# An attention kernel: loads of the first pass wait for the landing of the fourth load ahead of them

## Chip, cores and metric

The kernel runs on one core of one Trainium2 chip. The metric is the device time of one execution in microseconds (us); the time before is 235.31 us, the median of 3 runs (234.92 to 235.79). Engines are named as in the profile: PE multiplies matrices (PEld is its loading of weights), ACT applies functions, DVE is the vector engine, POOL and SP are the two engines that also issue most of the DMAs here. Transfers that POOL issues convert fp32 in memory to bf16 on the chip; those of SP copy without converting.

## What is computed

Softmax attention with one additive bias for all heads: 4 batches of 8 heads, 1024 positions, head size 64, all in fp32 at the interface.

```python
scores = scale * np.matmul(q, k.transpose(0, 1, 3, 2))
scores = scores + bias
scores_max = np.max(scores, axis=-1, keepdims=True)
attn = np.exp(scores - scores_max) / (np.sum(np.exp(scores - scores_max), axis=-1, keepdims=True) + 1e-8)
return np.matmul(attn, v).astype(np.float32)
```

## The kernel before

The 32 heads are worked on in 16 pairs. A query chunk is 128 rows, so each head has 8 chunks, and a unit of work (a "slot" in the code) is one chunk of one head: 256 slots. A slot has these steps.

- fill (lines 233 to 249): PE puts the 128 x 1024 scores of the slot into one of three places in PSUM, in 8 multiplications (L244). Where a chain of heads begins, the bias is put there first (L241, from `braw`); later heads of the same chunk add the difference of their scores to what stands there, so that the bias need not be added again. For this each pair keeps arrays `ko`, `qo` and `ke`, `qe` (k and q of one head, and of two heads one below the other, with the sign of one q turned).
- exponential (L258): ACT reads the place and writes `E` in bf16 (15 buffers). For 19 of the slots DVE does this instead in six steps (L275 to L295); 238 instructions of ACT remain.
- product with v (L312): PE multiplies `E` by `vall`, which holds v with a column of ones. Up to seven such results share a bank; then DVE divides them (L320, L322) and SP stores them (L689). There are two such banks, `xa` and `xb`, and the transposes use them too.

Heads go in two groups of 7 and 9 pairs. A group passes over its heads with chunks 0, 1 and 2 first, then with chunks 3 and 4, then with the rest. The first pass of the first group begins when the kernel begins: it takes pairs 0 to 6 one after the other, and each pair's k, q and v must have come by then.

How an input gets ready: a load brings k, q or v of one pair (each 256 KB as bf16; q of pairs 0 and 1 in two parts, the second named `qrest`) or 128 rows of the bias. PE transposes k and q (L191), DVE copies the result to `ko` or `qo` (L199, L201) and doubles it to `ke` and `qe` (L210, L212), or SP copies half of it with a DMA (L539). DVE copies v to `vall` (L493). There are 5 landing buffers for k, 5 for q, and 3 for v.

The order of all instructions is written out ahead by a planner in the kernel (from line 394 on), which carries an estimated time for each engine and picks what comes next. Each engine runs its list in order.

The loads: q, k and bias chunk 0 of the very beginning come by SP and ACT. POOL then issues seven loads directly (lines 352 to 358: bias chunks 1 and 2, k and q of pair 1, v of pair 0, k and q of pair 2). After these, line 767 calls `early` for 21 loads, in this order: k3, q3, v1, k4, q4, v2, k5, q5, v3, k6, q6, v4, v5, b3, q0, b4, v6, q1, b5, b6, b7 (b is a chunk of the bias, q0 and q1 are the second parts of q of pairs 0 and 1). `early` calls `issue`, which appends to the list `flight` the last element of what is loaded together with an estimated landing time. All 21 are issued by POOL ahead of everything that POOL does later.

Loads of pairs 7 to 15 come from `load` and `next_v`, by `issue` with `depth` LATE = 2 (3 for the last v loads). With a depth, `issue` puts a copy of one element ahead of the load (L468): it reads the last element of the load that many places back in `flight` and writes it to `tick`, so POOL waits until that load has landed.

```python
if 0 < depth <= len(flight):
    what, t = flight[-depth]
    nc.gpsimd.tensor_copy(tick[:], what)
```

With depth 0, as `early` calls it, there is no such copy.

Of the kernel before, what the change touches and what calls it, by code (L numbers as in the profile page):

```python
# [16 lines left out]
def kernel(  # L17
# [13 lines left out]
    nc = tc.nc  # L31
# [39 lines left out]
    tick = consts.tile([1, 1], BF)  # L71
# [263 lines left out]
    with tc.manual_schedule():  # L335
# [98 lines left out]
        flight = []  # L434
# [28 lines left out]
        def issue(at, cost, depth, load, pr, *a):  # L463

            nonlocal t_dma
# [3 lines that stand above are left out]
                at = max(at, t + 100)  # L469
            at = pool(at, 750)  # L470
            t_dma = max(t_dma + cost, at + 2200 + cost)
            flight.append((load(pr, *a), t_dma + 200))
            return t_dma + 200
# [17 lines left out]
        def move_v(pr):  # L491
            def run(t2):
                nc.vector.tensor_copy(vall[:, 2 * pr % VR:2 * pr % VR + 2, :, :D], lands[pr, "v"][:])  # L493
                v_at[pr] = t2 + 480 + L_DVE
                next_v(v_at[pr])
            dve_q.append((vland_at[pr] + VSLACK * (pr >= EARLY), 0.3, 480, run))


        def early(kind, pr):
            if kind == "k":  # L500
                raw_at[pr, 1, 0] = issue(0, E1, 0, load_k, pr) + SLACK
            elif kind == "q":
                cs = slice(0 if pr >= SPLIT else C0, NCH)
                raw_at[pr, 0, cs.start] = issue(0, E1 if pr >= SPLIT else E2, 0, load_q, pr, cs) + SLACK
            elif kind == "v":
                vland_at[pr] = issue(0, E1 if pr < 5 else E2, 0, load_v, pr)
                move_v(pr)
            else:
                bias_at[pr] = issue(0, E2, 0, load_b, pr)
# [257 lines left out]
        for x in ("k3", "q3", "v1", "k4", "q4", "v2", "k5", "q5", "v3", "k6", "q6", "v4", "v5", "b3", "q0", "b4", "v6", "q1", "b5", "b6", "b7"):  # L767
            early(x[0], int(x[1]))
# [71 lines left out]
```

## Time and profile before

| | |
|---|---|
| median of 3 runs | 235.31 us (234.92 to 235.79) |
| profiled execution, its own time | 235.12 us |
| its span, first to last instruction | 233.4 us |
| granted clock of PE, mean | 0.996 |
| DVE busy | 197.7 us, 290 instructions |
| POOL busy | 61.7 us, 99 instructions |
| exponentials on ACT (L258) | 238, 218.4 us busy |
| SP stores (L689), first pass, issue to landing | 2.6 / 6.2 / 8.6 us (min / median / max) |

How to read the profile: times count from the first instruction. A line of a timeline gives the start, the time from start to end of a row of merged instructions, the engine, the line of the code, the operation, what it writes and reads, the shape, how many there are, and in brackets the idle time of the engine before them with what ended it. "issue" as the one that ended it means that the profile shows nothing that the engine waited for. The digits after DMA are the mean busy share of the 16 DMA engines, in tenths, in 40 equal slices of the span. q0 is the queue of POOL's loads, q1 that of SP's and ACT's transfers, q8 that of instructions. Landing is when a DMA's data have arrived and its semaphore says so. POOL's DMA instructions are counted as busy while POOL writes their descriptors.

### The profile page before, as it was taken

How to read it: one execution, taken by the hardware profiler on the slowest of the kernel's cores; microseconds unless marked ns; L12 is line 12 of the kernel's file. 1: busy time of each engine (PE TensorE's matmuls, PEld its weight loads, DVE VectorE, ACT ScalarE, POOL GpSimd, SP SyncE). 2: the span in 40 equal slices, each digit the busy share in tenths (PEclk: the TensorE clock that was granted, in tenths of full speed). 3: DMA queues.
4: the chain of work that ended last, by engine and by line, in shares of the span. 5: the costliest groups of instructions: out<-in, count | busy, mean ns of one | idle time of the engine just before them, and what ended most of it. 6: DMA issues, size and time to landing. Idle time of an engine off the chain costs nothing.

```text
span 233.4 us, 10661 instructions
## 1 busy us (share of the span) xinstructions
PE 222.4 (95%) x4671; PEld 209.6 (90%) x4671; DVE 197.7 (85%) x290; ACT 221.6 (95%) x242; POOL 61.7 (26%) x99
## 2 busy tenths in 40 slices
PE   7899998899999999999999999999999999999992
PEld 2779997899999999998999999999998999999991
DVE  3576777599988998889989789899999899999991
ACT  3699999899999999999999999999999999999992
POOL 8754540276563636304254010000000000000000
PEclk9999999999999999999999999999999999999998
DMA  6999999899997999989899764111111112112112
GB/s 207 207 206 218 221 226 215 180 112 142 171 173 119 139 188 149 181 188 138 148 234 232 162 108 128 37 37 42 42 40 43 45 42 75 49 31 80 44 37 62
DMA packets 55645, 29.75 MB, mean 127 GB/s; under 512 B 31728, under 2 KB 51952, under 8 KB 55600
## 3 DMA queue, kind: packets, MB, share of 16 engines
q0 software_dynamic: 30336, 14.06, 48.5%
q1 hardware_dynamic: 24544, 14.33, 22.0%
q10 hardware_dynamic: 720, 0.69, 1.1%
q8 instruction: 36, 0.59, 1.1%
q14 instruction: 9, 0.07, 0.1%
HBM read 29.36 MB, written 8.39 MB: 162 GB/s over the span
## 4 chain that ended last, share of the span: by engine, by line
PE 44%; ACT 29%; issue 14%; DVE 5%; DMA 4%; SPq 2%; POOL 1%; DVEq 0%; ACTq 0%; POOLq 0%
ACT E L258 29%; PE pl L244 25%; PE po L312 12%; PE px L191 4%; DMA braw<-in_bias_dram 2%; PE pl L241 2%; SPq L689 2%; DMA out_dram<-ob 1%; DVE ob L322 1%; PE px L187 1%; DVE df L280 1%; DVE dy L275 1%; DVE dt L290 0%; DVE df L287 0%; DVE rs L320 0%
## 5 line engine op out<-in xcount | busy, mean ns | idle before, releaser
L258 ACT ACTIVATE E<-pl 128x1024 bf16<-128x1024 f32 (+1 forms) x238 | 218.4, 1119 | 3.4 <-PE pl L244 3.0
L312 PE MATMUL po<-vall,E 128*128 128x65 bf16 x1896 | 91.9, 194 | 1.7 <-ACT E L258 0.9
L312 PEld LDWEIGHTS <-E 128*128 128x128 bf16 x1896 | 77.4, 98 | 2.8 <-ACT E L258 1.2
L244 PE MATMUL pl<-qo,ko 128*128 128x128 bf16 x1024 | 76.9, 219 | 1.1 <-ACT E L258 0.6
L244 PEld LDWEIGHTS <-ko 128*128 128x128 bf16 x1160 | 69.4, 98 | 3.9 <-issue 0.9
L244 PE MATMUL pl<-qe,ke 128*128 128x128 bf16 x888 | 66.2, 219 | 2.1 <-issue 0.7
L244 PEld LDWEIGHTS <-ke 128*128 128x128 bf16 x888 | 53.4, 98 | 4.9 <-issue 1.3
L275 DVE TENSOR_SCALAR dy<-pl 128x1024 int32<-128x1024 f32 x19 | 23.2, 1221 | 4.4 <-PE pl L244 3.6
L322 DVE TENSOR_TENSOR ob<-po,rs 128x448 f32<-128x448 f32 (+2 forms) x39 | 23.2, 594 | 2.3 <-DVE rs L320 0.4
L284 DVE SCALAR_TENSOR_TENSOR dt<-df 128x1024 f32<-128x1024 f32 x19 | 23.2, 1220 | 0.3
L295 DVE SCALAR_TENSOR_TENSOR de<-dy,dt 128x1024 uint16<-128x1024 int32 x19 | 23.2, 1219 | 0.2
L287 DVE SCALAR_TENSOR_TENSOR df<-dt,df 128x1024 f32<-128x1024 f32 x19 | 23.1, 1220 | 0.1
L290 DVE SCALAR_TENSOR_TENSOR dt<-df,dt 128x1024 f32<-128x1024 f32 x19 | 23.1, 1219 | 0.1
L138 POOL DMA_DIRECT2D q<-in_q_dram x18 | 16.4, 911 | 7.0 <-DVE rs L320 5.4
L165 POOL DMA_DIRECT2D v<-in_v_dram x16 | 11.3, 705 | 20.9 <-DVE rs L320 9.9
L199 DVE COPY ko<-px 128x1024 bf16<-128x1024 bf16 (+1 forms) x16 | 10.8, 672 | 6.6 <-PE px L191 6.2
L201 DVE TENSOR_SCALAR qo<-px,sgn 128x1024 bf16<-128x1024 bf16 (+2 forms) x18 | 12.4, 686 | 4.2 <-PE px L191 2.6
L320 DVE RECIPROCAL rs<-po 128x7 f32<-128x7 f32 (+3 forms) x40 | 7.9, 197 | 7.2 <-PE po L312 7.0
L280 DVE TENSOR_SCALAR df<-dy 128x1024 f32<-128x1024 uint16 x19 | 13.3, 700 | 0.1
L241 PE MATMUL pl<-ident,braw 128*128 128x128 bf16 x136 | 11.6, 229 | 0.4 <-DMA braw<-in_bias_dram 0.3
L145 POOL DMA_DIRECT2D k<-in_k_dram x15 | 10.7, 713 | 2.2 <-DMA k<-in_k_dram 1.2
L241 PEld LDWEIGHTS <-braw 128*128 128x128 bf16 x136 | 9.9, 149 | 0.7 <-DMA braw<-in_bias_dram 0.5
(54 smaller groups left out, 119.9 us busy)
## 6 DMA issues: line engine op xcount, KB each, us to landing
v<-in_v_dram POOLq DMA_DIRECT2D x16, 256.0 KB, 6.1
k<-in_k_dram POOLq DMA_DIRECT2D x15, 256.0 KB, 6.3
out_dram<-ob SPq DMA_DIRECT2D x34, 96.0 KB, 3.6
ke<-ko SPq DMA_DIRECT2D x22, 128.0 KB, 4.7
out_dram<-ob SPq DMA_DIRECT2D x41, 64.0 KB, 2.3
q<-in_q_dram POOLq DMA_DIRECT2D x18, 128.0 KB, 4.9
qe<-q SPq DMA_DIRECT2D x17, 128.0 KB, 4.4
out_dram<-ob SPq DMA_DIRECT2D x67, 32.0 KB, 2.8
```

The costliest lines, as they stand in the source:

```text
L138: nc.gpsimd.dma_start(out=t[:, :, y, :], in_=(qf, kf)[x][pr][:, y].rearrange("p (c d) -> p c d", d=D))
L241: nc.tensor.matmul(to, braw[:, c, :].rearrange("p (kp kc) -> p kc kp", kc=NCH)[:, kc, :], ident8[:], start=i == 0, stop=False, skip_group_ ...
L244: nc.tensor.matmul(to, kk[:, kc, :], qq[:, c, :], start=False, stop=True, skip_group_check=True)
L258: nc.scalar.activation(e[:, i:i + n].rearrange("p b x -> p (b x)"), places[slots[s][0]][:, i:i + n].rearrange("p b x -> p (b x)"), ACTF.Ex ...
L275: w.tensor_scalar(t["y"][:], places[slots[s][0]].rearrange("p b x -> p (b x)"), scale * LOG2E * 65536.0, 127.0 * 65536.0, op0=ALU.mult, op ...
L280: w.tensor_scalar(t["f"][:], t["lo"], G / 65536.0, None, op0=ALU.mult)
L284: w.scalar_tensor_tensor(t["t"][:], t["f"][:], -G, t["f"][:], op0=ALU.add, op1=ALU.mult)
L287: w.scalar_tensor_tensor(t["f"][:], t["t"][:], Q, t["f"][:], op0=ALU.mult, op1=ALU.add)
L290: w.scalar_tensor_tensor(t["t"][:], t["f"][:], V, t["t"][:], op0=ALU.add, op1=ALU.mult)
L295: w.scalar_tensor_tensor(etile[s].bitcast(U16).rearrange("p c q -> p (c q)"), t["y"][:], 1.0 / 512.0, t["t"][:], op0=ALU.mult, op1=ALU.add)
L312: nc.tensor.matmul(po[:, j + i, :], etile[s][:, kc, :], vall[:, slots[s][2] % VR, kc, :], start=j + i + kc == 0, stop=kc == NCH - 1, skip_ ...
L322: nc.vector.tensor_tensor(ob[:, :n, :], po[:, :n, :D], rs[:, :n, :].to_broadcast([P, n, D]), op=ALU.mult)
```

## The change

In `early`, from the sixth call on, a copy of one element is put ahead of the load. It reads the last element of the load four places back in `flight`, so POOL waits until that one has landed before it issues the next. The order and the estimates of the planner are not touched.

```diff
         def early(kind, pr):
+            if len(flight) > 4:
+
+                nc.gpsimd.tensor_copy(tick[:], flight[-4][0])
             if kind == "k":
                 raw_at[pr, 1, 0] = issue(0, E1, 0, load_k, pr) + SLACK
```

`flight` holds only what went through `issue`; the seven loads of lines 352 to 358 are not in it.

## The prediction

> **What bounds the kernel now.** I read the page first, then the timeline of ACT, which shows what the end is made of.
>
> ```profile
> PE 222.4 (95%) x4671; PEld 209.6 (90%) x4671; DVE 197.7 (85%) x290; ACT 221.6 (95%) x242; POOL 61.7 (26%) x99
> ...
> DMA  6999999899997999989899764111111112112112
> ...
> q8 instruction: 36, 0.59, 1.1%
> ```
> ```profile
> 9.46 29.09 ACT L258 ACTIVATE E<-pl 128x512 bf16<-128x512 f32 x32 [0.67 <-PE pl L244]
> 38.86 1.94 ACT L258 ACTIVATE E<-pl 128x1024 bf16<-128x1024 f32 x2 [0.32 <-PE pl L244]
> 41.09 3.77 ACT L258 ACTIVATE E<-pl 128x1024 bf16<-128x1024 f32 x4 [0.29 <-ACT E L258]
> 45.51 4.89 ACT L258 ACTIVATE E<-pl 128x1024 bf16<-128x1024 f32 x5 [0.65 <-PE pl L244]
> 50.60 23.94 ACT L258 ACTIVATE E<-pl 128x1024 bf16<-128x1024 f32 x26 [0.20 <-PE pl L244]
> ```
>
> ACT makes 238 exponentials and sets the end: 26 in 23.94 us, the last one 1.02 long, is a pitch of 22.92 / 25 = 0.917 us, and 238 of them are 218 of the 233.4 us of the span. What can be won behind the start is only what ACT stands idle. Nearly all of that lies from 38.5 to 51 us. So I asked what PE did just before.
>
> ```profile
> 36.93 0.28 PEld L244 LDWEIGHTS <-ke 128*128 128x128 bf16 x5 [0.88 <-issue]
> 43.57 0.57 PEld L312 LDWEIGHTS <-E 128*128 128x128 bf16 x16 [0.94 <-issue]
> ```
> ```profile
> core 0: us, PE busy (x) PEld busy (x) DVE busy (x) ACT busy (x) POOL busy (x), PEclk, DMA share, GB/s
> 36.93:43.50 6.57, 5.86 (x127) 5.30 (x127) 3.98 (x9) 5.97 (x7) 0.00 (x0) 1.00 1.17 228
> ```
>
> PE's weight loads stop twice, the first time in the middle of a fill, with no semaphore to wait for ("issue"). Between the two stops lie 127 + 127 instructions and a wait or two, about 256. The page's instruction queue moved 0.59 MB in 36 packets, 16 KB each; 2 x 4671 instructions of PE over 36 packets is 260 to a packet. I read the stops as PE out of instructions: the next block comes late because it travels beside the loads. The trace's instruction packets of these two blocks begin at 34.48 and 41.25 and PE goes on 2.4 and 2.3 us after; counted in PE's instructions, the first five packets begin 18, 73, 90, 124 and 132 after a multiple of 256, later ones between 67 before and 66 after. From the two that stopped PE, 0.88 us at 24.5 ns each (6.3 us for 256) is 36, so some 90 is the latest that costs nothing.
>
> The loads themselves, POOL's timeline:
>
> ```profile
> 8.72 0.70 POOL L155 DMA_DIRECT2D q<-in_q_dram  x1
> 9.97 0.71 POOL L165 DMA_DIRECT2D v<-in_v_dram  x1 [0.55 <-DMA braw<-in_bias_dram]
> ...
> 13.07 0.70 POOL L165 DMA_DIRECT2D v<-in_v_dram  x1 [0.35 <-DMA v<-in_v_dram]
> ...
> 34.48 0.53 POOL L160 DMA_DIRECT2D braw<-in_bias_dram  x1 [0.78 <-DMA v<-in_v_dram]
> 44.41 0.18 POOL L468 COPY tick<-braw 1x1 bf16<-1x1 bf16 x1 [9.40 <-DMA braw<-in_bias_dram]
> 44.91 0.71 POOL L145 DMA_DIRECT2D k<-in_k_dram  x1 [0.32 <-PE pl L244]
> ```
>
> Already each load starts about 0.3 us behind the landing of the eighth ahead of it: v of pair 1 (9.97) behind the second bias load (3.84 + 5.8 = 9.7), v of pair 2 (13.07) behind v of pair 0 (5.77 + 7.0 = 12.8). Eight are in flight, each takes 9 to 11.7 us, and they land one by one: q of pair 3 at 8.72 + 9.3 = 18.0, the last bias load at 34.48 + 11.1 = 45.6, 19 landings in 27.6 us, 1.45 us each, 5.8 for four. The stage is bound by bandwidth (DMA share 1.17 above).
>
> **What the change adds.** `early` makes 21 loads; from the sixth (v of pair 2) on it puts a 1x1 copy on POOL first, so 16 copies, each with a wait for the landing four ahead. Nothing is removed or moved: the planner's times (`issue` with depth 0) are as before, so the order on PE, ACT, DVE and SP stays. It does act: v of pair 2 waits for 18.0 instead of 12.8 and starts some 5 us later, and so do the rest.
>
> Step 1, POOL's time. A copy takes 0.18 us free and up to 1.23 in later rows (59.62); with its wait met, copy and issue together took 0.82 (79.90 to 80.72) to 1.06 (73.54 to 74.60). That is under the 1.45 that a landing leaves, and POOL does nothing else here, so it costs nothing; without that cover it would be 16 x 0.3, about 5 us of later issue. The long copies ran beside DVE's two-input steps (59.59, 1.23 us, L290), which begin at 48.62; before, DVE's longest SBUF copies are 0.43 (L493), so at most 0.6 a copy. The Trainium skill (SBUF — State Buffer, section "SBUF: two separate sides") says that GpSimd and such DVE instructions lock each other out of a shared port pair for a whole instruction; the later rows agree, and by that rule too the sum here stays nothing.
>
> Step 2, when the loads land. A turn is: landing, copy, issue, landing. From landing to next issue the later stage took 0.6 (72.24 to 72.83) to 1.2 us (53.97 to 55.18); from a k load's issue to landing with at most two ahead 3.9 to 4.8. A turn is 4.5 to 6.0 against the 5.8 that four landings take anyway. I take 4.9 (the first pass has no long copies): the queue stays fed, and the landings stay where they are. Upper end: 0.2 late in each of four turns, 0.8 us at the last.
>
> Step 3, who waits. Behind the copies on POOL stand all later loads, the second stage's too (their first copy, 44.41, waits for a landing at 44.4). k and q have room: k of pair 4 lands at 20.7 and is transposed at 22.6, q of pair 6 31.0 and 37.3, k of pair 7 48.8 and 57.8; the biases land at 35.8 at the earliest and are used at 46.9. Only the v copies (L493) start as their load lands, and stand in DVE's order: 28.05 and 32.82 after idling 0.43 and 0.35. A v that is 0.2 to 0.4 late there (turns 1 and 2) is covered by the idle time DVE has just behind (0.43 before 28.91, 0.78 before 30.83, 0.33 before 34.98). I put down 0.1 us of ACT, 0 to 0.4.
>
> Step 4, what else uses the DMA engines. SP's half copies take
>
> ```profile
> DMA to landing us min/median/max: 5.2/6.3/8.3
> ```
> in the first pass (line 539, 14 to 45 us; eight loads in flight) and
> ```profile
> DMA to landing us min/median/max: 2.8/4.2/5.4
> ```
> from 46 to 90 us, with two or three. So what is in flight does delay other queues. The lateness of PE's blocks goes the same way: mean 87 instructions at eight, about -5 in the 14 from 44.8 to 122 us at two or three. No row shows four; a third of the way from -5 to 87 it is 26 on average, some 60 less than at eight, and 132 - 60 = 72 for the worst, under the 90. I take it that both stops of PE go, 1.82 us; the ends are none (0) and both. ACT's part of it: idle 0.32 + 0.29 + 0.65 = 1.26 by the list; by its pitch, the first exponential behind each gap costs some 0.1 more, 1.56. I take 1.4.
>
> Sum: 0.1 - 1.4 = -1.3 us on the profiled execution (235.12 us, span 233.4), 233.8; the median of the runs is 235.31, 0.19 higher, so 234.0.
>
> **Rivals.**
> B, nothing moves. The DMA engines have loads waiting at any moment, with four as with eight, and what another queue waits for may be its turn, not the depth. For it: SP's stores at 65 to 70 us took up to 6.3 us with few loads in flight; the 14.99 block was hardly late with eight. Against: the two medians above. PE stops as before: 235.3. The Trainium skill (DMA: Bandwidth & Descriptors, section "Queues, rings and completion order") speaks for it: each engine goes round its queues packet by packet, so a longer queue of loads would not hold up an instruction block longer. This trace disagrees so far as blocks came 1.5 us and more later than in the later stage, more than the 0.9 us that their own packet takes.
>
> C, slower: four in flight don't feed the engines. Place: v of pairs 3 to 5. It decides when a turn is over 5.8 us. With 1.2 from landing to issue and the 5.5 of the k load at 73.90, a turn is 6.7, 0.9 late a turn: v of pair 3 lands 0.9 late, of pairs 4 and 5 1.8. DVE stands at L493, the two evacuations behind it (33.50, 34.98) are late, PE has only two banks for them and the transposes, and ACT follows: 1.8 less the 0.33 of idle time, 235.3 + 1.5 = 236.8. Against it: the 1 us of room in step 2.
>
> **How the numbers follow.** The forecast 50%, 233.5 to 234.7; B 27%, 234.8 to 235.8; C 23%, 235.9 to 238. The likeliest gives 234.0. Range: down to 233.5 (both stops gone by the pitch, 1.56, and a little of the 0.3 us at 50.6), up to 236.4, half of C. Half a per cent, 1.18 us, is what a measurement can tell from no change: faster below 234.13 is most of the forecast, 40%; same the rest of it and B, 36%; slower C, with a little of B, 24%.
>
> **What would show it.** Right: no idle "issue" time on PE near 36.9 and 43.6; ACT without gaps from 10 to 50 us; loads in flight for 5 to 6 us instead of 10; the last bias load still landing near 45.6; SP's half copies under 6 us. Step 2 is wrong if that last landing is past 47 and L493 idles for over 1 us. Step 4 is wrong if PE's stops stay while the loads' time in flight halves. What I may have missed most easily is a new place for a late block.

## The result, and the profile after

The changed kernel is 0.5% slower: 235.93 us (median of 20 runs, 234.92 to 239.53) against 234.71 us of the kernel before (20 runs, 234.02 to 236.36); ratio 1.0048, 95% interval 1.0026 to 1.0069. A second series gave 236.03 against 235.05 us, ratio 1.0026 (1.0000 to 1.0052), the same way but with an interval that just reaches 1. Ratios here and below leave out executions more than 1.5% above the fastest of their kernel, so they are not exactly the quotients of the medians. The runs of the changed kernel spread far more than those of the kernel before. The profiled execution shown here took 234.92 us, one of its fastest, so its span of 232.8 us is no measure of the change; what can be read from it is where time is lost and won.

The timeline of ACT, changed kernel (start, length, engine, line, what, count, idle time before):

```profile
17.39 19.36 ACT L258 ACTIVATE E<-pl 128x1024 bf16<-128x1024 f32 x21 [0.41 <-PE pl L244]
37.28 3.80 ACT L258 ACTIVATE E<-pl 128x1024 bf16<-128x1024 f32 x4 [0.54 <-PE pl L244]
41.38 8.48 ACT L258 ACTIVATE E<-pl 128x1024 bf16<-128x1024 f32 x9 [0.30 <-ACT E L258]
```

PE's two stops without a semaphore are gone, and the gap of 0.65 us at 45.5 with them. In their place ACT idles 0.54 us at 37.28. (The 0.41 us at 17.39 stands behind q of pair 2, loaded ahead of all new waits; e7, which has none, idles 0.27 us there.) The timeline shows the chain that leads there, first DVE before, then DVE and PE after:

```profile
32.82 0.43 DVE L493 COPY vall<-v 128x1024 bf16<-128x1024 bf16 x1 [0.35 <-DMA v<-in_v_dram]
...
33.50 0.18 DVE L320 RECIPROCAL rs<-po 128x6 f32<-128x6 f32 x1
```

```profile
34.40 0.43 DVE L493 COPY vall<-v 128x1024 bf16<-128x1024 bf16 x1 [1.89 <-DMA v<-in_v_dram]
...
35.08 0.18 DVE L320 RECIPROCAL rs<-po 128x6 f32<-128x6 f32 x1
35.29 0.56 DVE L322 TENSOR_TENSOR ob<-po,rs 128x384 f32<-128x384 f32 x1
36.00 0.64 PE L191 MATMUL px<-ident,k 128*64 128x128 bf16 x16 [1.02 <-DVE ob L322]
```

Read the second from the bottom: PE stands 1.02 us before the transposes of k of pair 6, because the bank that they write is still to be evacuated; DVE evacuates late (35.08, 33.50 before), because it stood 1.89 us at the copy of v of pair 4, whose load lands at 34.4 (32.8 before). DVE stands again at v of pairs 5 and 6, 4.7 us at the v copies in all; it was 0.8 us.

The loads themselves, POOL's timeline of the changed kernel (L502 is the new copy):

```profile
24.08 0.18 POOL L502 COPY tick<-v 1x1 bf16<-1x1 bf16 x1 [0.38 <-DMA v<-in_v_dram]
24.53 0.70 POOL L145 DMA_DIRECT2D k<-in_k_dram  x1 [0.27 <-issue]
...
31.03 0.18 POOL L502 COPY tick<-k 1x1 bf16<-1x1 bf16 x1 [1.53 <-DMA k<-in_k_dram]
31.49 0.71 POOL L160 DMA_DIRECT2D braw<-in_bias_dram  x1 [0.28 <-issue]
```

A load starts 0.6 us behind the landing of the fourth ahead (23.95 to 24.53, 30.90 to 31.49) and is in flight for 4.5 to 8.4 us, 6.1 in the mean of the 16. A turn is 6.7 us. The landings say the same: q of pair 3 at 18.1, the last bias load at 49.4, 31.2 us for 19 landings, 6.6 us for four, where it was 5.8. Windows of the same 20 us, first before, then after (busy time by engine, granted clock, DMA share, GB/s):

```profile
26.00:46.00 20.00, 18.52 (x416) 17.01 (x414) 13.40 (x30) 18.75 (x21) 5.90 (x11) 1.00 1.12 215
```
```profile
26.00:46.00 20.00, 18.98 (x428) 17.72 (x426) 13.63 (x31) 19.16 (x22) 10.06 (x21) 1.00 1.13 195
```

All DMAs together move 195 GB/s instead of 215; from 26 to 30 us it is 181 against 218. The DMA share over the 20 us (1.13 against 1.12) does not show this: it adds up how long packets took, not what they carried.

### The profile page after: what moved, and what is told of

It reads as the page before. It is cut to its first block, busy times and chain, and to the rows that moved or that the text cites. A ratio compares the mean times of both kernels' runs of the same rounds, so it can differ in the third digit from the quotient of the medians.

```text
span 232.8 us, 10685 instructions
## 1 busy us (share of the span) xinstructions
PE 222.2 (95%) x4671; PEld 209.7 (90%) x4671; DVE 197.3 (85%) x290; ACT 221.5 (95%) x242; POOL 63.8 (27%) x115
## 4 chain that ended last, share of the span: by engine, by line
PE 34%; ACT 32%; issue 14%; DVE 8%; DMA 7%; POOL 3%; DVEq 0%; ACTq 0%; POOLq 0%
ACT E L258 32%; PE pl L244 20%; PE po L312 9%; DMA q<-in_q_dram 4%; PE px L191 3%; DMA v<-in_v_dram 3%; PE pl L241 2%; DVE ob L322 1%; DVE dt L290 1%; DVE df L287 1%; DVE dy L275 1%; DVE de L295 1%; DVE df L280 1%; DVE dt L284 1%; POOL k L145 1%
## 5 line engine op out<-in xcount | busy, mean ns | idle before, releaser
L312 PE MATMUL po<-vall,E 128*128 128x65 bf16 x1896 | 92.0, 194 | 0.9 <-ACT E L258 0.9
L312 PEld LDWEIGHTS <-E 128*128 128x128 bf16 x1896 | 77.4, 98 | 1.8 <-ACT E L258 1.2
L244 PE MATMUL pl<-qo,ko 128*128 128x128 bf16 x1024 | 76.8, 219 | 0.9 <-ACT E L258 0.4
L244 PEld LDWEIGHTS <-ko 128*128 128x128 bf16 x1160 | 69.4, 98 | 3.9 <-issue 0.6
L244 PE MATMUL pl<-qe,ke 128*128 128x128 bf16 x888 | 66.0, 219 | 1.3 <-DVE qe L212 0.5
L244 PEld LDWEIGHTS <-ke 128*128 128x128 bf16 x888 | 53.3, 97 | 3.9 <-DVE qe L212 0.6
L493 DVE COPY vall<-v 128x1024 bf16<-128x1024 bf16 x16 | 7.0, 437 | 4.7 <-DMA v<-in_v_dram 4.7
```

The source lines that it names most:

```text
L244: nc.tensor.matmul(to, kk[:, kc, :], qq[:, c, :], start=False, stop=True, skip_group_check=True)
L312: nc.tensor.matmul(po[:, j + i, :], etile[s][:, kc, :], vall[:, slots[s][2] % VR, kc, :], start=j + i + kc == 0, stop=kc == NCH - 1, skip_ ...
```

## The experiments

Each kernel was timed against the kernel before on the same chip. "ACT idle" is the sum of ACT's gaps over 0.15 us from 25 to 49 us in its one profiled execution, whose time stands beside it.

| run | waits of the first pass | median, before (us) | ratio (95%) | profiled us | ACT idle us |
|---|---|---|---|---|---|
| kernel before | none added | | | 235.12 | 1.25 |
| changed kernel | 4 ahead, 16 loads | 235.93, 234.71 | 1.0048 (1.0026 to 1.0069) | 234.92 | 0.84 |
| e1, e11, e12 | the same again | 236.03, 235.05 (e1) | 1.0026 (1.0000 to 1.0052) | 237.86, 235.59, 234.93 | 3.41, 1.36, 0.32 |
| e2 | 6 ahead | 235.01, 235.05 | 0.9997 (0.9975 to 1.0019) | 235.17 | 1.20 |
| e3 | 3 ahead | 239.32, 235.05 | 1.0187 (1.0148 to 1.0226) | 239.86 | 5.45 |
| e4 | 4 ahead, last 8 loads only | 233.95, 235.05 | 0.9963 (0.9940 to 0.9986) | 234.23 | 0.29 |
| e5 | copies without a wait | 234.89, 235.13 | 0.9987 (0.9965 to 1.0009) | 234.87 | 0.66 |
| e6 | 4 ahead, v copies later | 234.49, 235.13 | 0.9972 (0.9941 to 1.0002) | 234.31 | 0.51 |
| e7 | none, v copies later | 234.92, 235.13 | 0.9993 (0.9971 to 1.0016) | 234.65 | 0.94 |
| e8 | 3 ahead, last 8 loads only | 235.59, 235.13 | 1.0017 (0.9985 to 1.0049) | 235.39 | 1.28 |
| e9 | e4 and v copies later | 233.76, 235.02 | 0.9936 (0.9914 to 0.9958) | 233.76 | 0.00 |
| e10 | 5 ahead | 234.44, 235.02 | 0.9972 (0.9957 to 0.9988) | 234.44 | 0.30 |

**Is it the landings or the copies?** e1 repeats the changed kernel. e2, e3 and e10 keep the copies and move what they wait for; e5 keeps the copies and takes the added wait away.

```diff
-                nc.gpsimd.tensor_copy(tick[:], flight[-4][0])
+                nc.gpsimd.tensor_copy(tick[:], flight[-3][0])      # e3
+                nc.gpsimd.tensor_copy(tick[:], flight[-5][0])      # e10
+                nc.gpsimd.tensor_copy(tick[:], flight[-6][0])      # e2, from the seventh load on
+                nc.gpsimd.tensor_copy(tick[:], ident[:1, :1])      # e5
```

> The changed kernel once more, for a second profile of it. Theory A (late landings): with four in flight a load takes 5 to 7 us, four landings take about 6.6 us instead of 5.8, the v of pairs 4 to 6 land late, DVE stands at the v copies for 2 us or more in all, and the gain of PE's missing stops is more than spent; about 1 us slower than before. Theory B (the 16 copies on POOL cost it): the same time, but then DVE need not stand at the v copies. Both: no idle 'issue' time of 0.8 us on PE near 37 and 44 us.

> The same 16 copies, but each waits for the sixth load ahead. A: six landings take 8.7 us, one flight at most about 8, so the queue stays fed, the v land as before and the time is that of before or up to 0.7 us less (0 to -0.3%). B: as many copies, so as slow as the changed kernel, +0.5%.

> The same copies from the sixth load on, each waits for the third load ahead. A: a turn of three takes 0.6 + 5 us against 4.4, over 1 us late a turn, so the last landing comes 5 us or more later than before and the time is 2 to 5 us above before (+1 to +2%). B: as many copies, +0.5% as with four.

> The 16 copies at the same places on POOL, but each reads an element of the identity matrix that was ready at 2 us, so no wait is added and a load still starts behind the landing of the eighth ahead. A (late landings): the time of before, within 0.2%, and PE's two stops near 37 and 44 us stay. B (the copies cost it): +0.3 to +0.5%.

> From the sixth load on, the fifth ahead. A: five landings take 7.3 us; a turn is 0.6 us and a flight of 6 to 7, so the landings are late by 0 to 1 us: between the runs with four and six ahead, 0 to +0.2%, with PE's stops smaller than with six. If lateness came in only through the number of copies, +0.4% as with four.

The copies are not the cost: e5 has all 16 and e2 has 15, and neither is slower than before (e2 was expected to have 16; it begins one load later). What they wait for is. (Standing at v is not by itself a cost: DVE stood 2.5 us at the copies of v of pairs 3 to 6 in e5 and 2.1 in e10, but in pieces, and PE waited at most 0.25 us for it.) Three ahead, the windows and DVE's and ACT's timelines:

```profile
26.00:46.00 20.00, 15.70 (x324) 14.57 (x322) 10.85 (x25) 14.55 (x17) 8.80 (x20) 0.91 1.04 174
```
```profile
37.42 0.43 DVE L493 COPY vall<-v 128x1024 bf16<-128x1024 bf16 x1 [3.90 <-DMA v<-in_v_dram]
```
```profile
40.62 1.94 ACT L258 ACTIVATE E<-pl 128x1024 bf16<-128x1024 f32 x2 [3.18 <-PE pl L244]
```

Five ahead (e10), the same window:

```profile
26.00:46.00 20.00, 19.62 (x440) 18.23 (x437) 14.59 (x33) 19.66 (x22) 9.93 (x22) 1.00 1.12 217
```

174 GB/s with three, 195 with four (186 to 201 in its other profiles), 217 with five, 215 with six and, before, with eight. The last bias load lands at 55.1, 49.4, 45.9 and 45.5 us with three, four, five and six (45.6 before). The step lies between four and five: with five a flight is 5.8 to 7.5 us against the 7.3 that five landings take, and no load lands more than about 1 us late. For e10 I had expected at best the time of before; it is 0.28% faster. The three further profiles of the changed kernel (e1, e11, e12) have last landings at 51.1, 49.2 and 49.2 us; DVE stands 2.71, 1.99 and 1.07 us at v of pair 4, PE 1.84, 1.12 and 0.23 us for the evacuation behind it, and the executions took 237.86, 235.59 and 234.93 us. In these three the time goes with DVE's wait; the profile shown first (1.89 us at v of pair 4, 1.02 us of PE) took 234.92, so the order is not strict. That this wait makes the runs spread is likely, not shown.

> The changed kernel a third time, for one more profile. A: DVE stands at the copies of v of pairs 4 and 6 for over 1 us each, PE waits for the evacuation near 36 us for 1 us or more, and ACT's idle time behind it grows with that; where PE's wait is near 2 us, the granted clock may halve for some 3 us, as in the second profile.

> As the run before: the time over its fastest should follow PE's wait near 36 us.

e11 and e12 also corrected me on a point: PE's second stop is back in both, at 43.70 and 42.69 us.

```profile
43.70 0.57 PEld L312 LDWEIGHTS <-E 128*128 128x128 bf16 x16 [0.73 <-issue]
```

So four in flight does not always remove the stops. PE's idle time at the two block ends (L244 and L312, near 37 and 43 us) is 1.48, 0.78 and 0.92 us with eight in flight (before, e5, e7), 1.22 with six, 0.38 with five, and 0, 0, 0.56 and 0.44 in the four profiles of the changed kernel. In the two with none PE stood elsewhere just before, which also gives a block time to come. Each of these is a single profile, and before, e5 and e7 differ by 0.7 us with the same depth (in e5 the stops were expected to stay); what stands out is that six and eight lie above four and five.

**Is it DVE's standing at v?** In e6 and e7 the copies of v of pairs 3 to 6 are held back for four of the planner's DVE steps, or until a product with that v is emitted; e7 is the control without waits.

```diff
             def run(t2):
-                nc.vector.tensor_copy(vall[:, 2 * pr % VR:2 * pr % VR + 2, :, :D], lands[pr, "v"][:])
+                if 2 < pr < EARLY:
+                    held.append([4, pr])
+                else:
+                    copy_v(pr)
```

> The changed kernel, with DVE's copies of v of pairs 3 to 6 put some four steps later in DVE's order, so that the evacuations of PE's banks stand ahead of them. A: DVE no longer stands where PE waits for it, PE's wait of 1.0 to 1.8 us near 36 us and ACT's behind it go; with PE's two stops gone as well the time is 0.2 to 0.6% under before. If the late v hurt elsewhere (through the products with v, or the k and q that come late too), it stays at +0.3% or more.

> The kernel before with the same later copies of v, no wait added: the control for the run above. The v land in time here, so A expects the time of before, within 0.2%; if the later copies are a gain in themselves, this is faster by as much.

ACT's timeline in e6, same waits as the changed kernel:

```profile
9.69 30.37 ACT L258 ACTIVATE E<-pl 128x1024 bf16<-128x1024 f32 x33
40.57 8.69 ACT L258 ACTIVATE E<-pl 128x1024 bf16<-128x1024 f32 x9 [0.51 <-PE pl L244]
```

The gap near 37 us is gone although the loads land as late as in the changed kernel (last one at 48.7). What is left at 40.57 follows a wait of PE, 0.61 us at 38.88, for the second part of q of pair 0. The control alone changes nothing that can be measured. So the late v cost its time through its place in DVE's order, not through the products with v. The interval of e6 just reaches 1 against the kernel before; against the changed kernel (1.0048 and 1.0026) the difference is clear.

**The two effects apart.** e4 puts the waits only on the last eight loads, which DVE and PE come to late enough (v of pair 6 lands at 40.8 instead of 39.7 us, and DVE copies it at 41.1); e8 and e9 vary it.

```diff
         def early(kind, pr):
+            if len(flight) > 12:
+                nc.gpsimd.tensor_copy(tick[:], flight[-4][0])      # e4 and e9; [-3] in e8
```

> Four ahead again, but only from the fourteenth load (bias chunk 3) on, 8 copies: v of pairs 2 to 5 go as before. A: these v are on time, and the instruction blocks near 34 and 41 us meet fewer loads, so at least one of PE's two stops goes: 0.3 to 1.3 us faster than before (-0.1 to -0.5%). B: half the copies, half the loss: +0.25%.

> Three ahead, from the fourteenth load on only. A: the v of pairs 3 to 5 are on time; the loads behind land 2 to 4 us later than before, which bias chunks and the second part of q of pair 0 have room for, while the second part of q of pair 1 (transposed at 45.3, landing at 41.3 before) may just be late. The rest of PE's first stop shrinks. -0.3 to -0.7% against before; if q of pair 1 is late, about 0.

> Both parts that helped together: four ahead from the fourteenth load on, and the copies of v of pairs 3 to 6 later in DVE's order. If the late v of pair 6 still costs something with the tail alone, this is 0.1 to 0.3% under that run, -0.4 to -0.7% against before; if nothing is left to win there, the same as the tail alone (-0.2 to -0.5%).

In e4 the v of pairs 3 to 6 are on time (DVE stands 0.2 us in all), one stop of PE is gone, and the other is half as long:

```profile
36.83 0.28 PEld L244 LDWEIGHTS <-ke 128*128 128x128 bf16 x5 [0.42 <-issue]
```

e8 goes too far, and the gain is gone. The second part of q of pair 1, for which there was little room, is late, and v of pair 6 is too: DVE stands 3.54 us for it, and the evacuation behind it, for which PE waits as well, ends at 45.29. The q, which lands at 45.42, ends the wait last, but without it PE would have stood nearly as long.

```profile
45.46 0.31 PEld L191 LDWEIGHTS <-qrest 128*64 128x64 bf16 x10 [1.51 <-DMA qrest<-in_q_dram]
```

e9 has no gap at all from 17.4 to 49 us, and is the fastest of all, 0.64% under the kernel before:

```profile
17.44 31.58 ACT L258 ACTIVATE E<-pl 128x1024 bf16<-128x1024 f32 x34 [0.47 <-PE pl L244]
49.23 3.77 ACT L258 ACTIVATE E<-pl 128x1024 bf16<-128x1024 f32 x4 [0.20 <-PE pl L244]
```

**Outside the span.** Not all of the loss lies in the kernel's span. Time less span is 1.76 us (median of the runs) for the kernel before, 1.77 to 1.81 for e2, e4, e5, e7, e8 and e9, and 2.07 to 2.13 for the changed kernel (e1, e11 and e12 too), e3, e6 and e10. It is a step: the trace has 188 instructions of POOL, its waits counted, in every kernel of the second group, and 164 to 186 in those of the first. So 0.35 us of the loss, and as much of what e6 and e10 fell short of, goes with the length of POOL's list and not with the landings (e10's are those of before to within about 1 us). In the first series the median span of the changed kernel is 233.8 us, which is 0.85 us over 234.71 - 1.76; 0.85 and 0.35 make the 1.2 us that were measured. What happens in these 0.35 us is not in the trace, and no run varies the list's length alone; the cause stays open.

## Why the prediction was wrong

It forecast 234.0 us, 1.3 us faster than before; measured was 235.9, 1.2 us slower. The stated range reached 236.4 and holds the time, but only by way of the rival that came true, C, which had 23%, with its place (v of pairs 4 and 5, the evacuations behind them, PE's two banks) and the point from which it decides, a turn over 5.8 us. C's turn of 6.7 is what was measured, though made of 0.6 and 6.1 us, not of 1.2 and 5.5. Its price, 1.5 us over the time before, came near the 1.2 in part by luck: C counted neither the 0.35 us outside the span nor a gain from PE's stops.

- What bounds the kernel: right. In all profiles the 238 exponentials take 218.2 to 218.6 us, and profiled times follow ACT's idle time: 233.76 us at 0, 234.2 to 234.9 at 0.3 to 0.9, 235.1 to 235.6 at 1.2 to 1.4, 237.86 at 3.41, 239.86 at 5.45.
- Step 1, POOL's time: right inside the span (e5), and from landing to issue 0.6 us, as its lower row said. It missed the 0.35 us outside the span; no view of the trace before could show it.
- Step 2 failed: "I take 4.9 (the first pass has no long copies): the queue stays fed, and the landings stay where they are." The turn measured 6.6 to 6.7, the last landing came 3.8 us late against an upper end of 0.8. The term that was mis-sized is the flight, put at 3.9 to 4.8 us; measured it is 6.1 with three loads ahead. The range was taken from the first four k loads of the later stage (44.9 to 60.8 us); from 46 to 60 us all DMAs moved 128 GB/s, against 215 in the first pass. The five k loads behind them in the same trace of before, from 73.90 us on and with as few ahead, took longer, and the prediction used one of them for C alone:

```profile
DMA to landing us min/median/max: 5.3/5.5/7.1
```

With 0.6 us from landing to issue, 5.3 to 7.1 gives a turn of 5.9 to 7.7, over the 5.8 that four landings take: the 0.9 us of room was not there. The turns measured with three, four, five and six ahead are about 6.0, 6.7, 7.3 and 8.6 us (0.6 and the mean flight of the loads that wait), against 4.4, 5.8, 7.3 and 8.7 for as many landings. Five ahead had enough, four had not.
- Step 3 followed from it: 0.1 us of ACT became 0.54, 0.66 and 2.50 us behind PE's wait in three of the four profiles, and nothing in the fourth (e12). Which instruction waits, and who stands behind it on DVE, was right (e6).
- Step 4 was right in its direction and not in its size: with fewer loads in flight the stops shrink from 0.8 to 1.5 us at eight to 0 to 0.56 at four. That PE stops there for its next block of instructions is read from the packets' times; no run shows it by itself. SP's half copies fell only from 6.3 to 5.6 us in the median. The whole of it, no gap up to 49 us, came only in e9.
- Rival B fails as far as single profiles can tell: stops of 0.78 to 1.48 us in the four profiles with six to eight in flight, and of 0 to 0.38 us in e4, e9 and e10, where nothing else delayed PE, go with the depth. The Trainium skill (DMA: Bandwidth & Descriptors, section "Queues, rings and completion order") has the engines go round their queues packet by packet; that alone does not give this dependence. Another page of the Trainium skill (Runtime: NRT & Kernel Launch, section "Instruction fetch mechanics") says that instructions come in 16 KiB blocks of 256 and that crossing a block is mostly hidden. The blocks agree with the 256 instructions between the stops; hidden they were not, 0.70 and 0.77 us of PE before.

## What to carry to other kernels

Fewer loads in flight helped the others that share the DMA engines here (SP's half copies, PE's stops), but the depth must be taken from flights in the saturated stage itself, not from a quiet one, and needs a reserve: here five kept the bandwidth and four did not. Put the waits in front of loads that nobody waits for (e4), and look for an in-order engine that stands at a copy of late data ahead of work that others need (e6). A gain of about 1 us (e4) and a loss of nearly 2 (e6 against the changed kernel) hid in a change of 0.5%; only runs that removed one of them told them apart.

## What the runs showed of the hardware

A pause of PE of 1.0 to 1.3 us left its granted clock at 1.00 (the changed kernel, e8, e11), but one of 1.84 us in e1 (237.86 us) was followed by about 3.4 us at half, and so was one of 3.0 us in e3. Windows of e1:

```profile
37.00:38.00 1.00, 0.58 (x13) 0.61 (x15) 0.97 (x4) 0.03 (x1) 0.66 (x2) 0.75 1.06 134
38.00:39.00 1.00, 1.00 (x15) 0.83 (x12) 0.81 (x2) 0.00 (x0) 0.60 (x3) 0.50 0.65 58
39.00:40.00 1.00, 1.00 (x12) 1.00 (x10) 0.68 (x2) 0.48 (x1) 0.79 (x3) 0.50 0.85 145
40.00:41.00 1.00, 1.00 (x19) 0.80 (x17) 0.00 (x0) 1.00 (x2) 0.51 (x1) 0.55 0.98 206
```

The last column but two is the granted clock. ACT idled 2.50 us behind that pause, more than the pause itself, but 0.54 and 0.66 behind those of 1.02 and 1.12. By these two, an estimate of what stands behind 1.84 is some 1.4 us; the rest fits the half clock, which no run separates from the pause. The Trainium skill (TensorE: Matmul & The Clock Gate, section "Part 1: The HAM clock gate (the "warmup" mystery)") gives an idle window of about 3.4 us before the clock falls to half; here 1.84 us was enough, in one execution.
